# Retention and HGRN2 step: the fourth weight rows' T1, T3 and T4 splits tied behind pair two's token sums, pair three's tokens prepared one product later

## The chip, the cores and the metric

The kernel runs on one core of a Trainium2 chip. The metric is device time in microseconds (us). The kernel before takes 1026.99 us, the median of three runs (1026.68 to 1027.75). Engines are named as in the profile: PE is TensorE with its matmuls, PEld its weight loads, DVE VectorE, ACT ScalarE, POOL GpSimd, and SP the SyncE queue that issues most of the DMA transfers.

## The reference, cut to what matters

One layer with two parallel groups of four heads, retention and HGRN2, on 2048 prompt tokens and 8 sample tokens:

```
h = rmsnorm(x, norm_g)
p = (h @ w_in)                       # (2048, 1024) @ (1024, 8*512)
rq, rk, rv, rg, hq, hf, hi, hgate = split(p, 8)
rq = rotary(rq); rk = rotary(rk) * DK**-0.5
o_ret, s_ret = chunked_decay_recurrence(rq, rk, rv, log_gamma, s_ret)
o_hg,  s_hg  = chunked_decay_recurrence(silu(hq), kin(hf), hi, logf(hf), s_hg)
o = concat(head_rmsnorm(o_ret) * silu(rg), head_rmsnorm(o_hg) * silu(hgate))
y = rmsnorm(x + o @ w_out, final_norm_g)
```

All of it is float32. The work around the change is a part of `h @ w_in`: the 1024 columns of `w_in` that are called `w_v` (two column types of 512), for the first pairs of token chunks.

## The kernel before, in words

A float32 operand is split into a rounded high part (ACT writes it, L117) and the rest (DVE subtracts, L118). The helper is `hi_lo`. A product is three matmuls (high by high, high by low, low by high; `three`, L350) for each of four rows k of 128.

The 2048 tokens are 16 chunks of 128, taken as eight pairs. Pairs zero and one (`plain_k`) multiply the chunks straight, eight rows each. From pair two on (`v_pair`) a pair is one 2 by 2 block product with seven products instead of eight. Its token blocks are A11, A12, A21, A22 and four sums S1 to S4, and its weight blocks are B11, B21, B22 and four sums T1 to T4. The seven products run in the order of `CHAIN`: A11 B11, A12 B21, S2 T2, S1 T1, S3 T3, S4 B22, A22 T4. Products zero, two, four and six add up in one PSUM bank, called `pv2a` for pair two (`pv3a` for pair three). Its running sum is copied out by ACT in between: `s` after product zero and `u` after product two (L390), and `vo` after product four (L402), and PE may add the next product to the bank only when that copy is done. In the same way product three leaves its result in bank `pv2c`, ACT copies it (`p`, L390), and only then product five, S4 B22, may go on in that bank.

The weight sums come from `w_sums` and are made row by row in `wv_comb(0)` to `wv_comb(3)`: four DVE subtractions and four splits for each row. They stand between the end of pair zero and the plain products of pair one.

The tokens of a pair are made ready by `tok_ops` (L302 scales them by the norm, eight DVE instructions of 256 elements; L117 and L118 split them into `ab_h` and `ab_l`, first A11 as 512 elements, then A12 and A22 as 1024; L318 to L321 make the four sums, two in each tile `S`). `s_split(i, 0)` splits S2 and S3, `s_split(i, 1)` splits S1 and S4. Pair two's tokens are prepared beside pair one's last plain products, and pair i+1's tokens inside pair i: `after[n]` is a list of closures that the program emits behind product n. `stats_sum` squares rows of the prompt on ACT (L269, tiles `xn`, which an SP load brings). `decode_values_out` copies the sample tokens' values (`vd`, L615) and is emitted behind product three of pair two.

Each engine works through a fixed list of instructions, in order. The lists are laid down before the run by the framework, which takes the order of emission, the data dependences and its own priorities. The helper `behind(f)` ties what `f` emits: it stands behind the last instruction that DVE, ACT and SP have been given so far.

Of the kernel before, what the change touches and what calls it, by code (L numbers as in the profile page):

```python
# [14 lines left out]
ALU = mybir.AluOpType  # L15
# [26 lines left out]
def step_kernel(ctx, tc, a, out):  # L42
    nc = tc.nc
    pe, act, dve, pool, sp = nc.tensor, nc.scalar, nc.vector, nc.gpsimd, nc.sync
# [71 lines left out]
    def hi_lo(h, l, src):  # L116
        act.activation(h, src, AF.Copy)  # L117
        dve.tensor_tensor(l, src, h.bitcast(F32), op=ALU.subtract)  # L118

    def split(r, name):  # L120
        h = wp.tile([P, D], F32R, tag="wh", name=name + "h")
        l = wp.tile([P, D], F32R, tag="wl", name=name + "l")
        hi_lo(h, l, r)
        return h, l

    def behind(f):

        last = {}
        for i in reversed(nc.cur_bb.bb.instructions):
            if i.engine in (dve.engine, act.engine, sp.engine) and i.engine not in last:  # L130
                last[i.engine] = i
                if len(last) == 3:
                    break
        with ExitStack() as es:
            for i in last.values():
                es.enter_context(tc.issue_after(i))
            f()
# [64 lines left out]
    N_V = len(V_ORDER)  # L202
# [16 lines left out]
    b12 = [[wp.tile([P, 2, GW], F32R, tag="w" + t, name=f"B12{t}{n}") for n in range(2)] for t in "hl"]  # L219

    def wv(op, k):
        if op == "B12":
            return [t[k // 2][:, k % 2] for t in b12]
        return [t[:, k] for t in Bop[op]]
# [3 lines left out]
    def bank(shape, name, at=None):  # L228
        if at is not None:
            return ((ps_pj, ps_lv, ps_o)[at]).tile(shape, F32, tag=("pj", "lv", "o")[at], name=name)  # L230
        pl, tag = ((ps_pj, "pj"), (ps_lv, "lv"), (ps_o, "o"), (ps_tr, "tr"))[(0, 1, 2, 0, 1, 2, 3)[bank_n[0] % 7]]
        bank_n[0] += 1
        return pl.tile(shape, F32, tag=tag, name=name)
# [3 lines left out]
    def tok_load(i):  # L237
        p = TOK[i]
        xr[i] = [rawp.tile([P, 4, 2 * P], F32, tag="raw", name=f"xr{i}{j}") for j in range(2)]
        for j, r in enumerate(xr[i]):  # L240
            src = a_dram[p] if spooled(i) else a["x_t"][p]
            sp.dma_start(r, src[:, 4 * j : 4 * j + 4])
        if spooled(i):
            sraw[i] = [rawp.tile([P, 2, 4, P], F32, tag="raw", name=f"S{n}_{i}") for n in range(2)]
            for n, r in enumerate(sraw[i]):
                sp.dma_start(r, s_dram[p][n])

    def spooled(i):
        return i >= 2 * N_V or (i >= N_V and TOK[i] not in TOK[:2])

    def same(i):
        return 0 < i < len(TOK) and TOK[i] == TOK[i - 1]
# [6 lines left out]
    def stats_load(i, j):  # L259
        c = 2 * V_ORDER[i] + j  # L260
        st[i, j] = [vq.tile([P, GW], F32, tag="xn", name=f"xn{c}{h}", bufs=2) for h in range(2)]
        for h, r in enumerate(st[i, j]):
            sp.dma_start(r, a["x_prompt"][0, c * P : (c + 1) * P, h * GW : (h + 1) * GW])

    def stats_sum(i, j):
        if not j:
            st[i] = sm.tile([P, 4], F32, tag="ms", name=f"ms{V_ORDER[i]}")
        for h, r in enumerate(st[i, j]):
            act.activation(r, r, AF.Square, accum_out=st[i][:, 2 * h + j : 2 * h + j + 1])  # L269
# [7 lines left out]
    def stats_end(i):  # L277
        p, ms = V_ORDER[i], st[i]
        pool.tensor_tensor(ms[:, 0:2], ms[:, 0:2], ms[:, 2:4], op=ALU.add)
        rsqrt_mean(rs_all[:, 2 * p : 2 * p + 2], ms[:, 0:2], D, EPS)  # L280
# [3 lines left out]
    def spread(i):  # L284
        pt = ps_tr.tile([P, 2, P], F32, tag="tr", name=f"prs{i}")
        for j in range(2):
            c = 2 * TOK[i] + j
            pe.transpose(pt[:, j], rs_all[:, c : c + 1].to_broadcast([P, P]), ident)
        dst = vq.tile([P, GW], F32, tag="rq", name=f"rb{i}")[:, :256]
        dve.tensor_copy(dst, pt.rearrange("p a b -> p (a b)"))  # L290
        spread_to[i] = dst
# [36 lines left out]
    def s_split(i, m):  # L328
        hl = split(sraw[i][m].rearrange("p s k t -> p (s k t)"), f"s{i}{m}")
        for n, op in enumerate((("S2", "S3"), ("S1", "S4"))[m]):  # L330
            sop[i, op] = [
                x[:, n * 512 : n * 512 + 512].rearrange("p (k t) -> p k t", k=4) for x in hl
            ]
# [151 lines left out]
    wr = {}  # L485
# [16 lines left out]
    def w_sums(r0, r1):  # L502
        b11, b12, b21, b22 = (r[:, g] if hasattr(r, "shape") else r[g] for r in (r0, r1) for g in range(2))
        dve.tensor_tensor(b11, b12, b11, op=ALU.subtract)
        dve.tensor_tensor(b12, b22, b12, op=ALU.subtract)
        dve.tensor_tensor(b22, b22, b11, op=ALU.subtract)
        dve.tensor_tensor(b21, b21, b22, op=ALU.subtract)
        return ("T2", b22), ("T3", b12), ("T1", b11), ("T4", b21)

    def wv_comb(k):  # L510
        for op, r in w_sums(wr[k], wr[k + 4]):
            h, l = wv(op, k)
            hi_lo(h, l, r)

    def wg_load(n, k):
        for j, kk in enumerate((k, k + 4)):
            if n == 1 and (j or k % 2):
                tags = (f"zh{j}", f"zl{j}") if k % 2 else ("rk", "rg")
                wr[kk] = [vq.tile([P, GW], F32, tag=t, name=f"wgr{n}{kk}{t}") for t in tags]
                for g, r in enumerate(wr[kk]):  # L520
                    sp.dma_start(r, a[f"w_{n}"][kk, :, g * GW : (g + 1) * GW])
            else:
                wr[kk] = rawp.tile([P, 2, GW], F32, tag="raw", name=f"wgr{n}{kk}")
                sp.dma_start(wr[kk].rearrange("p g n -> p (g n)"), a[f"w_{n}"][kk])
# [106 lines left out]
    def plain_out(i, c, ty, ps):  # L631
        cc = 2 * V_ORDER[i] + c
        o = vq.tile([P, GW], F32, tag="vo", name=f"vp{cc}{ty}", bufs=3)
        act.activation(o, ps, AF.Copy, scale=rs_all[:, cc : cc + 1])
        v_out(0, cc, ty, o)

    def plain_k(i, ps, c, ty, k, first, last):
        three(ps, av(i, f"A{c + 1}{k // 4 + 1}", k % 4), wv(f"B{k // 4 + 1}{ty + 1}", k % 4), first, last)
# [46 lines left out]
    wv_comb(1)  # L685
    tok_load(2)
    wv_comb(2)
    wv_comb(3)
    for ty in (1, 0):
        for c in range(2):  # L690
            ps = bank([P, GW], f"pv1{c}{ty}")
            for k in range(KT):
                plain_k(1, ps, c, ty, k, k == 0, k == KT - 1)
            plain_out(1, c, ty, ps)
            if (c, ty) == (0, 0):
                spread(2)
                held = []
                stats_load(3, 0)
                stats_sum(3, 0)
                stats_load(3, 1)  # L700
                tok_ops(2, held, lambda: stats_sum(3, 1))
                stats_end(3)
                tok_load(3)
                for f in held:
                    f()
                s_split(2, 0)
    s_split(2, 1)
    stats_load(4, 0)
    dve.tensor_tensor(lbd, lbraw[:, :, 0], lbraw[:, :, 1], op=ALU.subtract)
    act.activation(lb, lbd, AF.Sigmoid)  # L710
# [208 lines left out]
    for i in range(2, n_tok):  # L919
# [13 lines left out]
        if same(i + 1):  # L933
            for op in ("S1", "S2", "S3", "S4"):
                sop[i + 1, op] = sop[i, op]
        elif i + 1 < n_tok:
            if not spooled(i + 1):
                after[1] += [lambda i=i: spread(i + 1)]
            tied = behind if i >= N_V - 1 else lambda f: f()
            late = 2 if same(i) else 0  # L940
            after[2 + late] += [
                lambda i=i, t=tied: t(lambda: tok_ops(i + 1)), lambda i=i, t=tied: t(lambda: s_split(i + 1, 0))
            ]
            after[4 + late // 2] += [lambda i=i, t=tied: t(lambda: s_split(i + 1, 1))]
        if i + 2 < n_tok and not same(i + 2):
            at = 5 if i % N_V > 2 else 2
            if same(i + 1):
                at = 6
            after[at] += [lambda i=i: tok_load(i + 2)]
# [10 lines left out]
        if m < 3:  # L960
# [9 lines left out]
            if j == 7:  # L970
                after[0] += [lambda m=m: behind(lambda: wg_decode_out(m))]
                for n, (_, op, _) in enumerate(CHAIN):
                    if m == 1 and op == "B11":
                        continue
                    at = {"B21": 0, "B22": 3}.get(op, n) if m == 1 else n
# [25 lines left out]
        if N_V <= i < 2 * N_V:  # L1001
            for n in range(12):
                for f, d in ((lambda n: behind(lambda: wo_pre_load(n)), 0), (lambda n: behind(lambda: wo_pre_split(n)), 2), (lambda n: behind(lambda: wo_pre_store(n)), 4)):
                    g = 7 + 4 * n + d
# [580 lines left out]
    levels, rest, late = [], [], []  # L1585
    tail = r_steps(N_V)
    tail_f = [lambda n=n: [f() for f in tail[n]] for n in sorted(tail)]
    for i in range(len(order)):
# [23 lines left out]
        late = rest  # L1612
# [272 lines left out]
    op = ctx.enter_context(tc.tile_pool(name="op", bufs=1))  # L1885
# [8 lines left out]
    for n in range(4):  # L1894
        i, st_ = ((4, 0), (4, 4), (5, 0), (5, 4))[n]
        wd_at[i] += [(st_, lambda n=n: wd_load(2 * n)), (st_, lambda n=n: wd_load(2 * n + 1))]
        i, st_ = ((4, 3), (5, 0), (5, 4), (6, 1))[n]
# [106 lines left out]
```

## Time and profile before

| what | value |
|---|---|
| median of 3 runs | 1026.99 us |
| profiled execution | 1027.67 us |
| its span, first to last instruction | 1025.8 us |
| PE busy | 1014.7 us, 99% |
| PEld busy | 842.6 us, 82% |
| DVE busy | 734.3 us, 72% |
| ACT busy | 551.5 us, 54% |
| POOL busy | 126.3 us, 12% |
| SP's DMA queue, share of 16 engines | 64.7% |

PE is busy nearly all the time, so the place to read is where it is not: the table of windows shows in which stretch PE has idle time, and the timeline shows which instruction of another engine ended it. A time in the timeline is microseconds from the start of the span.

### The profile page before, as it was taken

The numbers are of one execution on the slowest core, as the hardware profiler recorded it, in microseconds if no ns is written. First come the engines' busy times: TensorE is split into PE (matmuls) and PEld (weight loads), VectorE is DVE, ScalarE is ACT, GpSimd is POOL, SyncE is SP. The second block draws the span as 40 slices with busy tenths as digits, with TensorE's granted clock in tenths as the row PEclk, the third lists the DMA queues.
The fourth block names the chain that finished last, engine by engine and source line by source line (L and its number), as shares of the span: only waits on it lengthen the run. The fifth ranks groups of instructions, "written<-read, shape, count | busy, mean of one in ns | idle before, by whom it ended". The sixth has DMA issues, their size and how long they took to land. (4 is left out here: it accounts for less than half of the span.)

```text
span 1025.8 us, 21565 instructions
## 1 busy us (share of the span) xinstructions
PE 1014.7 (99%) x8372; PEld 842.6 (82%) x8372; DVE 734.3 (72%) x1353; ACT 551.5 (54%) x1211; POOL 126.3 (12%) x231
## 2 busy tenths in 40 slices
PE   9999999999999999999999999999999999999996
PEld 8767778887778888888888899898888878887775
DVE  5897665988675885566666758768768576668886
ACT  6864335735434665555564655666556476433242
POOL 0210101000000101111111100111022112301122
PEclk9999999999999999999999999999999999999999
DMA  8688998768999975677776697655963497566652
GB/s 288 219 303 312 371 341 310 302 251 315 319 323 307 363 250 165 190 244 240 226 239 193 220 328 260 205 178 205 288 205 133 136 350 234 180 254 205 231 183 103
DMA packets 152135, 255.63 MB, mean 249 GB/s; under 512 B 11520, under 2 KB 79376, under 8 KB 151904
## 3 DMA queue, kind: packets, MB, share of 16 engines
q1 hardware_dynamic: 142232, 225.01, 64.7%
q0 software_dynamic: 7440, 24.76, 6.3%
q10 hardware_dynamic: 2360, 4.47, 1.2%
q8 instruction: 66, 1.08, 0.4%
q14 instruction: 37, 0.30, 0.1%
HBM read 166.51 MB, written 87.69 MB: 248 GB/s over the span
## 5 line engine op out<-in xcount | busy, mean ns | idle before, releaser
L1054 PE MATMUL pjfh<-xh,w_h 128*128 128x512 f32 (+2 forms) x160 | 59.4, 371 | 0.0
L1054 PE MATMUL pjqh<-xh,w_h 128*128 128x512 f32 (+2 forms) x160 | 58.7, 367 | 0.0
L1248 ACT ACTIVATE kepth<-kh 128x1024 f32<-128x1024 f32 x24 | 25.4, 1060 | 60.4 <-DVE kh L1238 60.4
L1054 PE MATMUL pjfh<-xl,w_h 128*128 128x512 f32 (+2 forms) x160 | 55.7, 348 | 0.0
L1054 PE MATMUL pjqh<-xh,w_l 128*128 128x512 f32 (+2 forms) x160 | 55.7, 348 | 0.0
L1054 PE MATMUL pjfh<-xh,w_l 128*128 128x512 f32 (+2 forms) x160 | 55.6, 348 | 0.0
L1054 PE MATMUL pjqh<-xl,w_h 128*128 128x512 f32 (+2 forms) x160 | 55.6, 347 | 0.0
L1238 DVE TENSOR_TENSOR kh<-kh,fph 128x512 f32<-128x512 f32 x48 | 33.4, 696 | 22.7 <-PE plh L1268 19.7
L118 DVE TENSOR_TENSOR ab_l<-xr,ab_h 128x512 fp32r<-128x512 f32 (+1 forms) x40 | 37.4, 954 | 14.1 <-ACT ab_h L117 14.1
L783 DVE SCALAR_TENSOR_TENSOR obr<-por,omr,rg 128x128 f32<-128x128 f32 x64 | 18.0, 344 | 31.9 <-POOL omr L775 24.9
L773 ACT ACTIVATE obr<-por 128x128 f32<-128x128 f32 x64 | 16.9, 278 | 44.1 <-PE por L760 40.3
L117 ACT ACTIVATE ab_h<-xr 128x512 fp32r<-128x512 f32 (+1 forms) x40 | 32.3, 839 | 8.4 <-DVE xr L302 8.4
L1054 PEld LDWEIGHTS pjqh<-xh,w_h 128*128 128x128 f32 x160 | 30.4, 190 | 4.8 <-issue 1.2
L1054 PEld LDWEIGHTS pjfh<-xh,w_h 128*128 128x128 f32 x160 | 30.2, 189 | 4.1 <-issue 0.4
L1054 PEld LDWEIGHTS pjqh<-xh,w_l 128*128 128x128 f32 x160 | 30.1, 188 | 4.0
L1054 PEld LDWEIGHTS pjfh<-xh,w_l 128*128 128x128 f32 x160 | 30.1, 188 | 4.0
L409 ACT ACTIVATE vo<-vo 128x512 f32<-128x512 f32 x32 | 20.1, 629 | 23.7 <-DVE vo L403 10.5
L1241 DVE TENSOR_TENSOR qqh<-qqh,fph 128x512 f32<-128x512 f32 x48 | 32.8, 683 | 0.0
L1054 PEld LDWEIGHTS pjqh<-xl,w_h 128*128 128x128 f32 x160 | 30.2, 189 | 3.0
L1054 PEld LDWEIGHTS pjfh<-xl,w_h 128*128 128x128 f32 x160 | 30.2, 189 | 2.7
L302 DVE SCALAR_TENSOR_TENSOR xr<-xr,g_in,rb 128x256 f32<-128x256 f32 x64 | 26.9, 479 | 2.6 <-DMA xr<-in_x_t 2.4
L1681 PE MATMUL py<-woh,oc_h 128*128 128x512 f32 x64 | 26.7, 417 | 0.0
(1877 smaller groups left out, 3347.0 us busy)
## 6 DMA issues: line engine op xcount, KB each, us to landing
xr<-a_dram SPq DMA_DIRECT2D x24, 512.0 KB
S<-s_dram SPq DMA_DIRECT2D x24, 512.0 KB
xn<-in_x_prompt SPq DMA_DIRECT2D x32, 256.0 KB
xr<-in_x_t SPq DMA_DIRECT2D x16, 512.0 KB
a_dram<-xr SPq DMA_DIRECT2D x16, 512.0 KB
s_dram<-S SPq DMA_DIRECT2D x16, 512.0 KB
xr<-a_dram SPq DMA_DIRECT2D x32, 256.0 KB
or<-o_dram SPq DMA_DIRECT2D x16, 512.0 KB
```

The source lines that it names most:

```text
L117: act.activation(h, src, AF.Copy)
L118: dve.tensor_tensor(l, src, h.bitcast(F32), op=ALU.subtract)
L302: dve.scalar_tensor_tensor(r[:, k], r[:, k], g_in[:, kk : kk + 1], spread_to[i], op0=ALU.mult, op1=ALU.mult)
L409: act.activation(o, src, AF.Silu)
L773: act.activation(o[:, cc], po[:, h], AF.Square, scale=P ** -0.5, accum_out=ms[:, h : h + 1])
L783: dve.scalar_tensor_tensor(o[:, cc], po[:, h], ms[:, h : h + 1], rb_of[c, "g"][:, cc], op0=ALU.mult, op1=ALU.mult)
L1054: pe.matmul(ps, ww[:, kk], x[:, k, b0 : b0 + n], start=(k == 0 and i == 0), stop=(k == KT - 1 and i == 2),)
L1238: dve.tensor_tensor(kv[:, :, 0, :], kv[:, :, 0, :], two[:, :, 1:2].to_broadcast([P, nb, b]), op=ALU.mult)
L1241: dve.tensor_tensor(qv[:, :, 1, :], qv[:, :, 1, :], two[:, :, 0:1].to_broadcast([P, nb, b]), op=ALU.mult)
L1248: act.activation(ss[:, 512:], k[:, :HALF], AF.Copy)
L1681: pe.matmul(ps, o[:, kk], w[:, k % 4, i * 512 : (i + 1) * 512], start=(k == 0 and n == 0), stop=(k == KT - 1 and n == 2),)
```

## The change

Two things change. `wv_comb(3)`, the last row of weight sums, is cut in three: the first three subtractions and T2's split stay where they were, T1's split is tied behind `s_split(2, 0)`, and T3's split, the fourth subtraction and T4's split are tied behind `s_split(2, 1)`. And inside pair two, `tok_ops(3)` and `s_split(3, 0)` are emitted behind product three instead of product two, and the load of pair four's tokens behind product three, too. `s_split(3, 1)` stays behind product four.

```
+    def wv_comb_two(k):
+        b11, b12, b21, b22 = (r[:, g] for r in (wr[k], wr[k + 4]) for g in range(2))
+        dve.tensor_tensor(b11, b12, b11, op=ALU.subtract)
+        dve.tensor_tensor(b12, b22, b12, op=ALU.subtract)
+        dve.tensor_tensor(b22, b22, b11, op=ALU.subtract)
+        hi_lo(*wv("T2", k), b22)
+        def one():
+            hi_lo(*wv("T1", k), b11)
+        def two():
+            hi_lo(*wv("T3", k), b12)
+            dve.tensor_tensor(b21, b21, b22, op=ALU.subtract)
+            hi_lo(*wv("T4", k), b21)
+        return one, two
...
-    wv_comb(3)
+    comb_t1, comb_t34 = wv_comb_two(3)
...
                 s_split(2, 0)
+                behind(comb_t1)
     s_split(2, 1)
+    behind(comb_t34)
...
-            late = 2 if same(i) else 0
+            late = 2 if same(i) else 1 if i == 2 else 0
...
-            at = 5 if i % N_V > 2 else 2
+            at = 5 if i % N_V > 2 else 3 if i == 2 else 2
```

No instruction is added or taken away. The lists of PE, POOL and SP keep their order; those of DVE and ACT change between pair one and pair six.

On ACT, around pair two's first copy `s_2` out of bank `pv2a`, the list before was this (the T splits are not in it, they stand earlier):

```order
L117 ACTIVATE s20h<-S_2_710 128x1024
L117 ACTIVATE s21h<-S_2_711 128x1024
L390 ACTIVATE s_2_792<-pv2a 128x512
L269 ACTIVATE xn_763,ms_821<-xn_763 128x512
L117 ACTIVATE ab_h<-xr_719 128x512
L390 ACTIVATE u_2_840<-pv2a 128x512
```

and it is now:

```order
L117 ACTIVATE s20h<-S_2_703 128x1024
L117 ACTIVATE T1h<-wvr_292 128x512
L117 ACTIVATE s21h<-S_2_704 128x1024
L117 ACTIVATE T3h<-wvr_292 128x512
L390 ACTIVATE s_2_792<-pv2a 128x512
L269 ACTIVATE xn_763,ms_821<-xn_763 128x512
L117 ACTIVATE T4h<-wvr_294 128x512
L390 ACTIVATE u_2_840<-pv2a 128x512
```

T1h and T3h stand ahead of `s_2`, T4h behind it, and the first split of pair three's tokens (`ab_h`, 512 elements) has moved further down.

On ACT, from pair two's product two to its product six, before (`p_2` is the copy that S4 B22 waits for, `vo_914<-pv2a` the copy that A22 T4 waits for):

```order
L623 ACTIVATE rbd<-prsd 128x8
L269 ACTIVATE xn_764,ms_821<-xn_764 128x512
L117 ACTIVATE ab_h<-xr_720 128x1024
L390 ACTIVATE p_2_890<-pv2c 128x512
L117 ACTIVATE s30h<-S_3_856 128x1024
L615 ACTIVATE vd_892<-pvd 8x256 x2
L615 ACTIVATE vd_897<-pvd 8x256 x2
L402 ACTIVATE vo_914<-pv2a 128x512
```

and now:

```order
L640 ACTIVATE rbd<-prsd 128x8
L269 ACTIVATE xn_764,ms_821<-xn_764 128x512
L117 ACTIVATE ab_h<-xr_712 128x512
L390 ACTIVATE p_2_860<-pv2c 128x512
L117 ACTIVATE ab_h<-xr_713 128x1024
L117 ACTIVATE s30h<-S_3_876 128x1024
L632 ACTIVATE vd_892<-pvd 8x256 x2
L632 ACTIVATE vd_897<-pvd 8x256 x2
L402 ACTIVATE vo_914<-pv2a 128x512
```

`p_2` has moved ahead of the large `ab_h`, and both `ab_h` stand behind the second `xn`.

On DVE, from the copy `rb` that starts pair three's tokens to the split of their first sums, before:

```order
L290 COPY rb_819<-prs_816 128x256
L302 SCALAR_TENSOR_TENSOR xr_719<-xr_719,g_in,rb_819 128x256 x4
L302 SCALAR_TENSOR_TENSOR xr_720<-xr_720,g_in,rb_819 128x256 x2
L118 TENSOR_TENSOR ab_l<-xr_719,ab_h 128x512
L302 SCALAR_TENSOR_TENSOR xr_720<-xr_720,g_in,rb_819 128x256 x2
L624 TENSOR_TENSOR pk<-pk,rbd 128x64
L318 TENSOR_TENSOR S_3_857<-xr_719,xr_720 128x512
L320 TENSOR_TENSOR S_3_856<-xr_719 128x512
L319 TENSOR_TENSOR S_3_856<-S_3_857,xr_719 128x512
L118 TENSOR_TENSOR ab_l<-xr_720,ab_h 128x1024
L321 TENSOR_TENSOR S_3_857<-xr_720,S_3_856 128x512
L118 TENSOR_TENSOR s30l<-S_3_856,s30h 128x1024
```

and now:

```order
L290 COPY rb_819<-prs_816 128x256
L118 TENSOR_TENSOR T4l<-wvr_294,T4h 128x512
L302 SCALAR_TENSOR_TENSOR xr_712<-xr_712,g_in,rb_819 128x256
L641 TENSOR_TENSOR pk<-pk,rbd 128x64
L302 SCALAR_TENSOR_TENSOR xr_712<-xr_712,g_in,rb_819 128x256 x3
L302 SCALAR_TENSOR_TENSOR xr_713<-xr_713,g_in,rb_819 128x256 x4
L118 TENSOR_TENSOR ab_l<-xr_712,ab_h 128x512
L318 TENSOR_TENSOR S_3_877<-xr_712,xr_713 128x512
L118 TENSOR_TENSOR ab_l<-xr_713,ab_h 128x1024
L319 TENSOR_TENSOR S_3_876<-S_3_877,xr_712 128x512
L320 TENSOR_TENSOR S_3_876<-xr_712 128x512
L321 TENSOR_TENSOR S_3_877<-xr_713,S_3_876 128x512
```

The two sums S2 and S3 (L319, L320), which `s30h` on ACT reads, have moved from ahead of the large `ab_l` to behind it.

## Rows read from the trace of the kernel before

**Rows 1.** Windows: stretch, busy us of PE, PEld, DVE, ACT, POOL; clock, DMA share, GB/s.
```profile
50.00:76.27 26.27, 24.16 (x103) 17.90 (x101) 24.54 (x45) 16.69 (x35) 3.91 (x7) 1.00 0.86 300
76.27:100.00 23.73, 23.73 (x123) 18.52 (x126) 17.41 (x28) 10.13 (x19) 1.08 (x3) 1.00 0.86 304
100.00:1000.00 900.00, 899.80 (x7788) 751.74 (x7781) 639.84 (x1186) 479.28 (x1052) 108.70 (x190) 1.00 0.73 250
```
**Rows 2.** Timeline of PE: start, duration, engine, line, operation; in brackets idle before, releaser.
```profile
56.67 0.50 PE L350 MATMUL pv2a<-wv_h,ab_h 128*128 128x512 f32 x1 [0.90 <-ACT ab_h L117]
...
60.66 0.50 PE L350 MATMUL pv2b<-wv_h,ab_l 128*128 128x512 f32 x1 [0.24 <-DVE ab_l L118]
...
63.79 0.50 PE L350 MATMUL pv2a<-T2h,s20h 128*128 128x512 f32 x1 [0.33 <-ACT s L390]
...
73.25 0.50 PE L350 MATMUL pv2c<-B22h,s21h 128*128 128x512 f32 x1 [0.64 <-ACT p L390]
...
76.27 0.50 PE L350 MATMUL pv2a<-T4h,ab_h 128*128 128x512 f32 x1
```
**Rows 3.** Timeline of ACT, pair two.
```profile
55.99 0.63 ACT L117 ACTIVATE ab_h<-xr 128x512 fp32r<-128x512 f32 x1 [1.57 <-DVE xr L302]
56.53 0.61 ACT L269 ACTIVATE xn<-xn 128x512 f32<-128x512 f32 x1
...
57.14 0.61 ACT L269 ACTIVATE xn<-xn 128x512 f32<-128x512 f32 x1
...
58.18 1.06 ACT L117 ACTIVATE ab_h<-xr 128x1024 fp32r<-128x1024 f32 x1 [0.33 <-DVE xr L302]
...
61.24 1.06 ACT L117 ACTIVATE s20h<-S 128x1024 fp32r<-128x1024 f32 x1 [1.43 <-DVE S L319]
62.21 1.04 ACT L117 ACTIVATE s21h<-S 128x1024 fp32r<-128x1024 f32 x1
63.16 0.58 ACT L390 ACTIVATE s<-pv2a 128x512 f32<-128x512 f32 x1
...
71.04 0.63 ACT L269 ACTIVATE xn<-xn 128x512 f32<-128x512 f32 x1 [2.48 <-DMA xn<-in_x_prompt]
...
71.67 1.04 ACT L117 ACTIVATE ab_h<-xr 128x1024 fp32r<-128x1024 f32 x1
72.62 0.58 ACT L390 ACTIVATE p<-pv2c 128x512 f32<-128x512 f32 x1
73.10 1.05 ACT L117 ACTIVATE s30h<-S 128x1024 fp32r<-128x1024 f32 x1
74.05 1.54 ACT L615 ACTIVATE vd<-pvd 8x256 f32<-8x256 f32 x4
75.61 0.60 ACT L402 ACTIVATE vo<-pv2a 128x512 f32<-128x512 f32 x1
```
**Rows 4.** Timeline of DVE, the end of the weight sums and pair two.
```profile
50.20 0.69 DVE L506 TENSOR_TENSOR wvr<-wvr,wvr 128x512 f32<-128x512 f32 x1
...
53.84 0.41 DVE L290 COPY rb<-prs 128x256 f32<-128x256 f32 x1
...
59.39 1.22 DVE L118 TENSOR_TENSOR ab_l<-xr,ab_h 128x1024 fp32r<-128x1024 f32 x1
60.53 0.68 DVE L319 TENSOR_TENSOR S<-S,xr 128x512 f32<-128x512 f32 x1
...
65.67 2.65 DVE L302 SCALAR_TENSOR_TENSOR xr<-xr,g_in,rb 128x256 f32<-128x256 f32 x6
...
70.97 0.68 DVE L319 TENSOR_TENSOR S<-S,xr 128x512 f32<-128x512 f32 x1
72.75 1.23 DVE L118 TENSOR_TENSOR ab_l<-xr,ab_h 128x1024 fp32r<-128x1024 f32 x1 [1.10 <-ACT ab_h L117]
```
**Rows 5.** Timeline of SP's DMA issues, around the second `xn` of pair two.
```profile
59.84 0.32 SPq L344 DMA_DIRECT2D v_dram<-vp  x1
...
62.34 1.03 SPq L263 DMA_DIRECT2D xn<-in_x_prompt  x1
```

## The prediction

> **What bounds the kernel now.** I read the windows first. From 76.27 to 100 us PE is busy all 23.73 us, and from 100 to 1000 us it is busy for 899.80 of 900 [rows 1]. So the kernel is bound by PE, and nothing behind 76.27 us can swallow a delay of PE or hide a gain: what moves the last product of pair two, A22 T4, moves the end by as much. From 50 to 76.27 us PE is busy for 24.16 of 26.27, so 2.11 us is all the idle time there.
>
> Then PE's timeline. The reader is to see four waits: 0.90 us until pair two's first `ab_h`, 0.24 until `ab_l`, 0.33 until the copy `s`, 0.64 until the copy `p` [rows 2]; they add up to that 2.11. The fifth row, A22 T4 at 76.27, has no idle time in brackets, and yet its first matmul takes the 0.50 us that the four which had waited take. ACT's copy `vo` out of the same bank ends at 75.61 + 0.60 = 76.21, just ahead of it [rows 3]. That copy releases T4 already now, with almost nothing to spare.
>
> Last the timelines of ACT and DVE, to see what each of these waits hangs on.
>
> **The change part by part.** Nothing is added or removed. The sum is over the moment at which A22 T4 starts.
>
> *Fourth weight row.* T1l, the fourth subtraction, T3l and T4l leave DVE ahead of the copy `rb` of 53.84; that is four of about 0.60. DVE does not win all of 2.4 us, since T2l now has to wait for ACT's T2h, which starts when L506 ends (50.20 + 0.69) and takes about 0.62, like the `ab_h` of that size. T2l then starts at about 51.6, and `rb` 0.60 later, at 52.2 instead of 53.84: 1.6 us earlier, or 1.3 if the `xn` ahead of T2h on ACT holds it a little [rows 3, 4]. The first `ab_h` comes at 54.4 to 54.7 instead of 55.99, before PE needs it: the wait of 0.90 goes. The large `ab_h` (58.18) stands behind the `xn` of 57.14, whose landing time the trace doesn't show; it ran without waiting. If it lands as early as ACT can use it, `ab_h` gains 1.6, if not before 57.14, then 0.43. I take 1.2, nearer the early end, since ACT found it landed [rows 3]. The large `ab_l` (59.39), L319 (60.53) and `s20h` (61.24) follow, so about 1.3 us earlier each.
>
> *The same splits, put back.* On ACT, T1h and T3h now stand ahead of `s`. One split of 512 costs 56.53 - 55.99 = 0.54, both 1.08 [rows 3]. So `s` is at 63.16 - 1.3 + 1.08 = 62.9 and PE takes S2 T2 at 63.5 to 63.6 instead of 63.79. Of more than 1 us won, about 0.2 to 0.3 is left there (bounds from the paragraph above: 0.65 lost, 0.6 won). T1l, T3l, the subtraction and T4l land on DVE between `s20l` and pair three's L302, three of them behind `s21l`; `pk` comes forward to behind the first L302 and waits some 0.4 us for `rbd`, which waits for PE. ACT's T1h leaves `s21l` 0.8 of the 1.3 us, and three of 0.60 follow: L302 starts at 65.67 - 0.8 + 1.8 = 66.7, and its eight end at about 70.3 (the six take 2.65, so eight 3.5, and a little for `pk`) [rows 4].
>
> *Pair three's tokens one product later.* The copy `p` now has only `xn` and the small `ab_h` ahead of it. Call X the moment at which ACT can start that second `xn`, whose load the trace shows to have ended ACT's wait at 71.04. Then `p` starts at X + 0.63 + 0.54, which is 0.41 us less behind X than now (72.62 - 71.04 = 1.58), and PE's wait of 0.64 mostly goes. But what is late next is `vo`, and with it A22 T4. `s30h` reads both S2 and S3, which were made at 70.97 and before, ahead of the large `ab_l` [rows 4]; so it could run at 73.10, right behind `p` [rows 3]. Now they stand behind that `ab_l`, which waits for the large `ab_h`, which stands behind `p`. `s30h` waits for all this, and behind it on ACT in strict order stand the four `vd` and then `vo`. Step by step from X, with the start-to-start distances of [rows 2 to 4]:
>
> - `xn` 0.63, small `ab_h` 0.54, `p` 73.10 - 72.62 = 0.48: the large `ab_h` starts at X + 1.65;
> - from it to the large `ab_l` on DVE, 72.75 - 71.67 = 1.08: X + 2.73;
> - `ab_l` 60.53 - 59.39 = 1.14, then L319 0.60 and L320 0.68, and 0.03 to ACT: `s30h` starts at X + 5.18 (now X + 2.06);
> - `s30h` 0.95, the four `vd` 1.56, and from `vo` to T4 76.27 - 75.61 = 0.66: A22 T4 starts at X + 8.35 (now X + 5.23).
>
> So at the same X the change costs 3.12 us at T4. X itself comes earlier: SP issues in order, and the store `vp` at 59.84 waits for ACT's `vp`, which stands right behind the large `ab_h`. The four issues behind it and the load of `xn` at 62.34 follow [rows 5]; SP's order is kept. All move by the 1.2 us that `ab_h` gains. The load takes 8.7 us to land, behind transfers that are shifted alike, so I take X = 71.04 - 1.2 = 69.84 and T4 at 78.2: 1.9 us late. Bounds: X not earlier at all, 3.1 us late; X so early that DVE's L302 decide (they end at 70.3, so the large `ab_h` starts at 70.35, which is X = 68.7), T4 at 77.05, 0.8 us late. Loads that follow on SP are issued some 0.5 us later than now and leave the queue freer, so I lean a little to the early side: 1.8 us.
>
> *What else is late.* `s30l`, `s31h` and `s31l` come 2 to 3 us later than now; PE asks for `s30` only in pair three's product two, which stands behind the whole of A22 T4 and two more products of 2.73 us, over 8 us; so they cost nothing. In pair three the order of `s40h` and `vo` is turned round, too, but there the tokens are not displaced: 0.95 of `s40h` stands against the 2.73 us (twelve matmuls of 0.23) of product five between `vo`'s input and T4. POOL, PE and SP keep their order and cost nothing.
>
> The profiled execution took 1027.67 us (span 1025.8 and 1.87 around it), so the sum for it is 1027.67 + 1.8 = 1029.5. That execution is 0.68 above the median of 1026.99; from the median the forecast is 1028.8 us. Its own range by the bounds is 1027.8 to 1030.1.
>
> **The rivals.**
>
> *A. The waits just go.* If `xn`, `ab_h` and the sums come so early that `vo` is done in time, PE loses nothing: all of 2.11 us [rows 1, 2], giving 1024.9. For it: these four are the only waits, and each of them is relieved. Against it: `s` gets 1.08 us of splits in front, and T4 is now held by a chain of 8.35 us behind X, so X would have to be below 66 and L302 to end 3 us before 70.3. Chance 0.06.
>
> *B. A wash.* X comes early enough, and `pk` and T4l hold DVE less than I think, so that T4 starts within 0.7 us of 76.27; 1026.5 to 1027.7, at the middle 1027.1. It decides where X is under 68.7 and L302 end before 70.2. Not slower, in any way that can be told. Chance 0.13.
>
> *C. PE's clock.* The granted clock is 1.00 (2.4 GHz) in all stretches shown [rows 1], also around the waits, of which the longest is 0.90 us. Here PE would stand idle from the end of S4 B22 (at about 75.3, that is 76.27 less the wait of 0.64 and the 0.3 won before) to T4 at 78.2, some 3 us in one piece, which this trace nowhere shows behind its start. If the grant fell to 1.2 GHz there and stayed so for one product, that product, 76.27 - 73.25 = 3.0 us with its start [rows 2], would take twice as long: 3.0 us more, 1031.8. Chance 0.07. The Trainium skill, "TensorE: Matmul & The Clock Gate", Part 1, says that an idle PE falls to half its clock and has to be kept busy for a time before the full one is given back; no row of before shows a fall.
>
> **How the numbers follow.** Forecast 0.74, A 0.06, B 0.13, C 0.07. A measurement of this kernel can tell about 0.2%, or 2.05 us, from no change. The forecast's 1.8 us lies just inside; of its range 0.8 to 3.1 I put 0.45 above 2.05 and 0.55 below. Slower: 0.74 x 0.45 + 0.07 = 0.40. Same: 0.74 x 0.55 + 0.13 = 0.54. Faster: 0.06. The range from 1027.0 to 1030.4 holds the forecast with its bounds and most of B, and leaves out A and C, 0.13 in all.
>
> **What would show it right or wrong.** In the profile of the changed kernel the first `ab_h` of pair two should start at 54.3 to 54.8 with no wait of PE before it; `s` at 62.5 to 63.3; PE should lose its wait for `p`; and in its place one long wait of 2 to 4 us should stand before A22 T4, released by ACT's `vo`, with `s30h` released by DVE's L320 two to three us later than at 73.10. The second `xn` should end ACT's wait near 69.8; T4 should come 8.35 us behind it. PE should have no wait behind T4. I am wrong if no wait stands before T4, if `s30h` starts before the large `ab_l`, or if PE waits anywhere in pair three or four.

## The result, and the profile after

The changed kernel takes 1031.2 us, the median of 18 runs (1027.36 to 1032.95), against 1027.65 us for the kernel before in the same series (18 runs, 1025.43 to 1030.48). The ratio is 1.0031, with a 95% interval of 1.0022 to 1.0041: slower by 3.2 us (the two medians differ by 3.55). Slower was forecast, but by 1.8 us and to no more than 1030.4.

The profiled execution hides most of it: 1028.26 us, span 1026.4, only 0.6 us above the profiled one of before. Its windows (columns as in [rows 1]):

```profile
50.00:76.27 26.27, 23.62 (x104) 18.45 (x102) 23.31 (x41) 15.20 (x30) 3.25 (x4) 1.00 0.88 316
76.27:100.00 23.73, 22.84 (x112) 18.14 (x113) 18.02 (x30) 11.78 (x24) 2.24 (x6) 1.00 0.93 320
100.00:1000.00 900.00, 899.55 (x7787) 751.20 (x7786) 640.01 (x1186) 478.13 (x1048) 107.36 (x188) 1.00 0.73 249
```

PE's idle time from 50 to 100 us has grown from 2.11 to 3.54 us, and it is one wait now. PE's whole list of waits in the profile after (who waited for whom: total, times, longest, in us):

```profile
PE pv2a L350 <- ACT vo L402: 3.5, 1, 3.5
PE wu L84 <- POOL ones L78: 1.1, 1, 1.1
PE pv8a L350 <- ACT u L390: 0.3, 1, 0.3
```

The four waits of [rows 2] are gone in this trace, and in their place stands one of 3.5 us, by the copy `vo`, before A22 T4. PE's timeline of after has it as its only row with idle time between 54 and 106 us; it is the row that answers to the last one of [rows 2]:

```profile
77.16 0.50 PE L350 MATMUL pv2a<-T4h,ab_h 128*128 128x512 f32 x1 [3.54 <-ACT vo L402]
```

ACT's timeline of after, the rows that answer to [rows 3]:

```profile
52.96 0.63 ACT L117 ACTIVATE ab_h<-xr 128x512 fp32r<-128x512 f32 x1 [0.52 <-DVE xr L302]
...
55.30 1.04 ACT L117 ACTIVATE ab_h<-xr 128x1024 fp32r<-128x1024 f32 x1
...
61.20 0.57 ACT L390 ACTIVATE s<-pv2a 128x512 f32<-128x512 f32 x1
...
68.82 0.63 ACT L269 ACTIVATE xn<-xn 128x512 f32<-128x512 f32 x1 [3.27 <-DMA xn<-in_x_prompt]
...
69.45 0.62 ACT L117 ACTIVATE ab_h<-xr 128x512 fp32r<-128x512 f32 x1
69.97 0.58 ACT L390 ACTIVATE p<-pv2c 128x512 f32<-128x512 f32 x1
70.45 1.05 ACT L117 ACTIVATE ab_h<-xr 128x1024 fp32r<-128x1024 f32 x1
73.99 1.06 ACT L117 ACTIVATE s30h<-S 128x1024 fp32r<-128x1024 f32 x1 [2.50 <-DVE S L320]
74.95 1.53 ACT L632 ACTIVATE vd<-pvd 8x256 f32<-8x256 f32 x4
76.51 0.60 ACT L402 ACTIVATE vo<-pv2a 128x512 f32<-128x512 f32 x1
```

and DVE's, which answer to the last two of [rows 4], now the other way round:

```profile
71.53 1.22 DVE L118 TENSOR_TENSOR ab_l<-xr,ab_h 128x1024 fp32r<-128x1024 f32 x1
72.67 0.68 DVE L319 TENSOR_TENSOR S<-S,xr 128x512 f32<-128x512 f32 x1
73.27 0.68 DVE L320 TENSOR_TENSOR S<-xr 128x512 f32<-128x512 f32 x1
```

The reader is to see the chain of the prediction, link by link: `xn` at X = 68.82, the large `ab_h` at X + 1.63, `ab_l`, L319, L320, then `s30h` at X + 5.17 after an idle ACT of 2.50 us that L320 ended, the four `vd`, `vo`, and A22 T4 at 77.16 = X + 8.34.

But T4 is only 0.89 us later than the 76.27 of before, and the windows hold the full clock. That explains the 0.6 us of this execution and not the 3.2 of the median. What differs is the mean granted clock, which each run lists: 0.998 to 0.999 in the profiled run and one other of the 18, 0.995 to 0.997 in sixteen.

### The profile page after: what moved, and what is told of

Read it like the earlier page. It is cut to its first block, busy times and chain, and to the rows that moved or that the text cites. A ratio compares the mean times of both kernels' runs of the same rounds, so it can differ in the third digit from the quotient of the medians.

```text
span 1026.4 us, 21572 instructions
## 1 busy us (share of the span) xinstructions
PE 1014.1 (99%) x8372; PEld 843.4 (82%) x8372; DVE 734.6 (72%) x1353; ACT 551.9 (54%) x1211; POOL 127.8 (12%) x231
## 4 chain that ended last, share of the span: by engine, by line
PE 92%; DMA 3%; DVE 2%; issue 1%; ACT 1%; SPq 0%; POOL 0%; POOLq 0%; ACTq 0%; DVEq 0%
PE po L350 11%; PE pjqh L1073 9%; PE pjfh L1073 8%; PE py L1700 4%; PE pv L350 4%; PE plh L1287 2%; PE par L764 1%; PE puh L1156 1%; PE pur L771 1%; PE por L777 1%; PE poh L1172 1%; PE por L779 1%; DMA T3l<-ws1T 1%; PE poh L1174 1%; PE pv20a L350 1%; PE pv22a L350 1%
```

## The experiments

Theory 1, clock: the piece of 3.5 us in which PE stands idle makes the clock fall in most runs, which costs some 2 to 3 us on top of the late T4. Theory 2, wait: T4 comes later in most runs than in the profiled one, by a later `xn`. Theory 3: the moved instructions of pairs three to six cost it. In all ratios below, the kernel before is timed in the same series.

**The changed kernel again**, without an edit.

> The changed kernel once more. Clock theory: the wait of 3.5 us before A22 T4 costs about 1 us by itself (0.9 in the first profile), and in most runs the granted clock falls to half behind it for some microseconds; then runs with a mean clock of 0.995 to 0.997 take 2 to 4 us more than those at 0.998 or 0.999, and a profile of such a run shows a stretch behind 75 us with a granted clock well under 1. Wait theory: the wait itself is longer in most runs because the xn load lands later (2 to 3 us more), the clock of all stretches stays at 1.00, and the time follows the wait.

Measured: 1030.6 us (12 runs), ratio 1.0027 [1.0018, 1.0035]. The clock is 0.994 to 0.997 in ten runs and 0.998 in two; all 29 runs of before lie at 0.998 or 0.999. The profiled run is one at 0.998 (1027.99 us): wait 3.5 us, X at 69.50, T4 at 77.84. So the wait has the same length again, and the clock goes with the time by and large, but the trace of a fall was still missing.

**The wait filled on PE, lightly.** `fill` is emitted behind product five.

```
+    def fill():
+        pt = ps_tr.tile([P, P], F32, tag="tr", name="fill")
+        for _ in range(7):
+            pe.matmul(pt, ones, ones, start=True, stop=True)
...
+            after[5] += [fill]
```

> The changed kernel with seven matmuls of 128x128 by ones, about 2.8 us, put on PE between S4 B22 and A22 T4; they compute nothing that is used. Clock theory: A22 T4 starts when it did (8.35 us behind xn), PE is kept busy, the mean clock is 0.998 to 0.999 in all runs, and the time is 0.5 to 2 us above before, not 3.2. Wait theory: the fill changes nothing, ratio 1.003 again. A third theory, that the moved instructions of pairs three to six cost it: 1.003 too.

Measured: 1030.11 us (11 runs), ratio 1.0029 [1.0017, 1.0041]. A miss for theory 1 as put. The fill took 1.7 us and not 2.8 and left PE a wait of 1.97 us; six of the eleven runs still list 0.996 or 0.997, where theory 1 had expected none; its profile is of a run at 0.999. By the ratio alone this run would have spoken for theories 2 and 3, so the fill had to be made longer and denser.

**The wait filled densely.** The same place, product five once more into a spare bank that nobody reads:

```
+        for k in range(4):
+            (xh, xl), (wh, wl) = av(2, "S4", k), wv("B22", k)
+            for x, w in ((xh, wh), (xh, wl), (xl, wh)):
+                pe.matmul(pt, x, w, start=True, stop=True)
```

> The changed kernel with twelve matmuls of 128x512 (2.7 us), product five over again into a spare bank that nobody reads, between S4 B22 and A22 T4. They leave PE under 1 us of the wait of 3.5. Clock theory (PE's idle piece brings the clock down): all runs at a mean clock of 0.998 or 0.999, T4 where it was, so the time is that of the changed kernel's undisturbed clock, 1028 to 1029, ratio 1.0005 to 1.0015. Other theory (the clock falls for a reason that is not PE's idle time): most runs at 0.995 to 0.997 and ratio 1.0025 to 1.003 as for the changed kernel.

Measured: 1029.3 us (11 runs), ratio 1.0013 [1.0005, 1.0022]. The clock is 0.998 or 0.999 in eight runs (1028.8 us in the mean) and 0.997 in three (1030.0), where theory 1 had expected all at 0.998 or 0.999. PE's row of T4 in its profile:

```profile
77.83 0.50 PE L350 MATMUL pv2a<-T4h,ab_h 128*128 128x512 f32 x1 [0.72 <-ACT vo L402]
```

T4 starts where it does without the fill (X there is 69.48, so X + 8.35). Up to T4 the lists of ACT and DVE are those of the changed kernel, and what differs is that PE was busy; behind T4 some of their instructions in pairs three to seven have changed places, without a wait of PE there. Over half of the loss is gone. Theory 2 would have left it at 1.003, and so would theory 3 if those places don't matter.

**The wait made longer.** Each of the four `vd` copies is made three times.

```
+                for _ in range(3):
+                    act.activation(t[:, n * 256 : n * 256 + 256], pvd[0][32 * j : 32 * j + NB], AF.Copy)
```

> The changed kernel with each copy of the sample values made three times, which puts some 3.3 us more of ACT's work ahead of vo; the wait before A22 T4 grows from 3.5 to about 6.9 us. Clock theory: the clock falls in every run, also in the profiled one, whose windows behind the wait show a granted clock of about half for some microseconds; mean clock 0.994 to 0.996, time 3.3 us over that of the changed kernel's runs with a fallen clock: 1034 to 1035, ratio 1.006 to 1.007. Without an effect of the clock: 1027.6 + 1 + 3.3 = 1032, ratio 1.004, all windows at 1.00.

Measured: 1033.87 us (4 runs), ratio 1.0057 [1.0035, 1.0079], clock 0.993 to 0.995 in all four. The interval holds the 1.004 without an effect of the clock, too, so here the windows decide and not the time. The wait is 6.4 us, not 6.9, since five of the twelve `vd` copies have come out behind `vo`. PE stands idle from 72.56 to 78.99. The clock is 1.00 until 76 us, 0.51 in the microsecond behind that, 0.50 until 82 and 1.00 again from 83, some 4 us after PE had taken up its work.

**The changed kernel profiled three times more**, to see the fall in its own trace.

> The changed kernel, one look, to catch the fall of the clock in its own trace. Clock theory: where the mean clock is 0.995 to 0.997, the windows behind the wait show a stretch of 5 to 8 us with a granted clock of about 0.5, PE takes twice as long for the products in it, and A22 T4 starts where it does in the looks without a fall (X + 8.35, 77 to 78.2). Other theory: in such a run T4 starts 2 us later and all windows are at 1.00.

> The same look at the changed kernel once more, since not every run shows the fall; both theories expect what they expect of the first look.

> A third look at the changed kernel, for the same reason; both theories expect what they expect of the first look.

Measured: 1030.9, 1030.55 and 1028.08 us, clock 0.995, 0.997 and 0.998. T4 starts at 77.38, 77.46 and 77.70, each 8.34 or 8.35 us behind its X (69.04, 69.12, 69.35), and the wait is 3.5 us in each. PE's row of T4 in the first of the three traces, and its windows (columns as in [rows 1]):

```profile
77.38 0.80 PE L350 MATMUL pv2a<-T4h,ab_h 128*128 128x512 f32 x1 [3.55 <-ACT vo L402]
```

```profile
74.00:75.00 1.00, 0.00 (x0) 0.00 (x0) 0.78 (x2) 0.79 (x1) 0.00 (x0) 1.00 0.56 229
75.00:76.00 1.00, 0.00 (x0) 0.00 (x0) 0.70 (x1) 0.96 (x4) 0.00 (x0) 1.00 1.02 418
76.00:77.00 1.00, 0.00 (x0) 0.00 (x0) 1.00 (x3) 0.96 (x3) 0.00 (x0) 0.68 1.01 414
77.00:78.00 1.00, 0.62 (x2) 0.52 (x3) 0.95 (x2) 1.00 (x2) 0.00 (x0) 0.50 1.10 266
78.00:79.00 1.00, 1.00 (x4) 0.81 (x3) 0.75 (x2) 1.00 (x4) 0.00 (x0) 0.50 1.01 201
...
82.00:83.00 1.00, 1.00 (x7) 0.27 (x9) 0.00 (x0) 0.00 (x0) 0.00 (x0) 0.50 1.04 404
83.00:84.00 1.00, 1.00 (x17) 0.26 (x9) 0.38 (x1) 0.00 (x0) 0.00 (x0) 0.91 0.77 295
```

Windows of the third trace:

```profile
76.00:77.00 1.00, 0.00 (x0) 0.00 (x0) 1.00 (x2) 0.96 (x3) 0.00 (x0) 1.00 1.03 422
77.00:78.00 1.00, 0.30 (x1) 0.30 (x2) 0.94 (x3) 0.98 (x3) 0.00 (x0) 1.00 1.07 340
78.00:79.00 1.00, 1.00 (x6) 0.79 (x5) 0.74 (x2) 1.00 (x2) 0.00 (x0) 1.00 1.35 229
```

The column to read is the granted clock, third from the end. In the first trace PE stands idle from 73.83; the clock is 1.00 (2.4 GHz) until 76, 0.68 in the row behind that, then 0.50 (1.2 GHz) until 83. In the third, with as long a wait, it stays at 1.00. PE is busy in all of the first trace's rows from 78 us on, yet starts four matmuls between 78 and 79 where the third starts six, and T4's first matmul takes 0.80 us instead of 0.50. The 0.68 and 0.91 put the two turns at about 76.4 and 83.2 us. From T4 at 77.38 to 83.2 that is 5.8 us of work at half clock, half of which is lost: 2.9 us by this estimate. The spans of the first and third trace differ by 1029.1 - 1026.3 = 2.8. In the second trace the clock falls at about 77.4, as T4 starts, and is back by 80.9, after 3.4 us; by the same estimate that costs 1.7. A later row bears both out: ACT's last copy of pair six, `vo` (L407), which PE releases. In the first, the second and the third trace:

```profile
165.10 0.60 ACT L407 ACTIVATE vo<-pv6a 128x512 f32<-128x512 f32 x1 [3.90 <-PE pv6a L350]
```

```profile
164.11 0.60 ACT L407 ACTIVATE vo<-pv6a 128x512 f32<-128x512 f32 x1 [3.89 <-PE pv6a L350]
```

```profile
162.81 0.60 ACT L407 ACTIVATE vo<-pv6a 128x512 f32<-128x512 f32 x1 [3.89 <-PE pv6a L350]
```

It starts 87.7 us behind T4 in the first, 86.6 in the second and 85.1 in the third, as in the other two traces in which the clock held. So the fall has cost 2.6 and 1.5 us up to there.

That is rival C, seen directly, and theory 2 is out: T4 doesn't start later in the two traces with a fall. Over the 33 runs of the changed kernel the clock fell in 28 (0.997 or less), which took 1031.0 us in the mean, and held in 5, with 1028.3. The line at 0.997 is not sharp: 2 of the 71 runs of before list 0.997, too, at 1026.8 and 1025.4 us. The six such runs of the changed kernel take 1030.9 us, like the rest of the 28; for the filled kernels the listed mean is all there is.

Theory 3 falls by the same runs. The instructions of pairs three to six are moved in all 33, and yet five take 1028.3 us; and the 85.1 us from T4 to the end of pair six are not more than the 85.2 in the trace of before:

```profile
161.50 0.60 ACT L407 ACTIVATE vo<-pv6a 128x512 f32<-128x512 f32 x1 [1.71 <-PE pv6a L350]
```

**One part alone: the later tokens.** The fourth row is back to `wv_comb(3)`.

> Only pair three's tokens are moved one product later; the splits of the fourth weight row stay where they were before the change. The lists of ACT and DVE come out nearly as before: s30h reads sums made ahead of the large ab_l again, and p stands behind the large ab_h. If the wait before A22 T4 is a matter of both parts together: no long wait, T4 at 76 to 76.5, the four waits of before, clock 0.998 to 0.999, ratio 0.999 to 1.001. If the later tokens make the wait by themselves: T4 at 78, ratio 1.002 to 1.003.

Measured: 1026.89 us (11 runs), ratio 0.9998 [0.9988, 1.0008], clock 0.998 or 0.999. T4 at 75.55, earlier than the 76 to 76.5 expected, as X is at 70.33; it is X + 5.22, as before. Of the four waits two are there, `s` with 0.32 us and `p` with 0.99. By itself this part changes nothing: ACT's list comes out as before, and DVE's but for `pk`.

**One part alone: the splits.** The two numbers that move pair three's tokens and load are back.

```
-            late = 2 if same(i) else 1 if i == 2 else 0
+            late = 2 if same(i) else 0
...
-            at = 5 if i % N_V > 2 else 3 if i == 2 else 2
+            at = 5 if i % N_V > 2 else 2
```

> Only the splits of the fourth weight row are moved; pair three's tokens are prepared where they were before the change. The order on ACT that comes out has vo ahead of s30h, behind three of the four vd and the large ab_h: T4 at X + 4.3, no wait of over 0.5 us before it, ratio 0.998 to 0.999 (1 to 2 us under before). If the loss came from the splits in front of the copy s: S2 T2 at 64.5 or later and a ratio of 1.001 or more.

Measured: 1025.84 us (12 runs), ratio 0.9979 [0.9967, 0.9991], clock 0.998 or 0.999. S2 T2 at 61.66, T4 at 73.65 with hardly a wait (X is 69.36, so X + 4.29), `s` 0.69 us late. ACT's rows:

```profile
71.53 1.04 ACT L117 ACTIVATE ab_h<-xr 128x1024 fp32r<-128x1024 f32 x1
72.59 0.38 ACT L632 ACTIVATE vd<-pvd 8x256 f32<-8x256 f32 x1
73.00 0.60 ACT L402 ACTIVATE vo<-pv2a 128x512 f32<-128x512 f32 x1
73.49 1.05 ACT L117 ACTIVATE s30h<-S 128x1024 fp32r<-128x1024 f32 x1
```

`vo` has come out ahead of `s30h`. So the splits win what they can win, and the wait belongs to the pair of edits and to neither alone.

**The order of `vo` and `s30h` turned round.** The changed kernel with one number altered:

```
-            after[3] += [lambda: behind(decode_values_out)]
+            after[4] += [lambda: behind(decode_values_out)]
```

> The changed kernel with the sample values' copies (vd) emitted behind product four instead of three; that turns the order of vo and s30h on ACT round, too. Both theories on T4: no wait of over 0.5 us before A22 T4, T4 at about 74.5 to 75.5, no fall of the clock, and the time 1 to 2 us under before (ratio 0.998 to 0.999). If the loss lies in pairs three to six: ratio 1.001 to 1.003.

> The kernel with the sample values' copies one product later, again, for its time: ratio 0.9965 to 0.9990 as before, mean clock 0.998 or 0.999 in all runs, A22 T4 at 73 to 75 without a wait. If the first 6 runs were luck: 0.999 to 1.000.

Measured: 1025.27 us (6 runs), ratio 0.9976 [0.9963, 0.9989], and in a second series 1025.87 us (11 runs), 0.9985 [0.9976, 0.9994]; the clock is 0.998 or 0.999 in all 17. `vo` follows the large `ab_h` at once, and T4 starts without a wait (first series):

```profile
70.21 1.05 ACT L117 ACTIVATE ab_h<-xr 128x1024 fp32r<-128x1024 f32 x1
71.16 0.59 ACT L402 ACTIVATE vo<-pv2a 128x512 f32<-128x512 f32 x1
73.76 1.06 ACT L117 ACTIVATE s30h<-S 128x1024 fp32r<-128x1024 f32 x1 [2.01 <-DVE S L320]
```

```profile
73.22 0.39 PE L350 MATMUL pv2a<-T4h,ab_h 128*128 128x512 f32 x1
```

This version beats both kernels, by 1.2 to 2.3 us under before. It is no test of theory 3: from 84 us on its lists of ACT and DVE are again those of the kernel before, as they are with the splits alone.

**One step more: the splits behind `s`.** As the kernel before it, and both calls tied behind product zero of pair two:

```
+            after[0] += [lambda: behind(comb_t1), lambda: behind(comb_t34)]
```

> As the kernel with the sample values' copies one product later, and the splits of the fourth row tied behind pair two's product zero, so that the copy s stands ahead of T1h and T3h on ACT. Theory: the wait of 0.5 us before S2 T2 goes as well, T4 at 72.8 to 74.5, ratio 0.997 to 0.998, 0 to 0.6 us under that kernel. Rival: T1l or T4l come too late for products three and six, or pk and L302 get later and the wait before S4 B22 grows; ratio 0.998 to 0.999.

Measured: 1025.84 us (11 runs), ratio 0.9982 [0.9970, 0.9993]. The wait for `s` is gone, T4 comes at 73.05, but the time is not under that of the version above. The list of waits shows one place where it is lost again:

```profile
PE pv7a L350 <- ACT vo L402: 0.9, 1, 0.9
```

Pair seven's A22 T4 waits for its own `vo` here; it did so by 1.35 us with the splits alone, and by 0.94 in the second profile of the version above. In the first profile of that version it doesn't wait, with T4 of pair two as early as 73.22. There ACT had stood idle before this `vo` for 0.57 us until the store `v_dram<-vo` had ended, in the second for 1.80. So when PE runs ahead, that copy takes a part back in some runs; it wasn't tried further.

## Why the prediction was wrong, point by point

*The wait that takes the others' place: right.* The forecast was one wait of 2 to 4 us before A22 T4, released by `vo`, with `s30h` held by L320 behind the large `ab_l`. It is there, 3.5 us long, in every trace of the changed kernel. T4 was put at X + 8.35; five traces show 8.34 or 8.35.

*X: right in kind, too small in size.* It was taken 1.2 us earlier, at 69.84, and came 1.5 to 2.2 us earlier, at 68.8 to 69.5; the large `ab_h`, on which that 1.2 rests, came 2.9 us earlier in the profile after (55.30). T4, forecast for 78.2, came at 77.2 to 77.8. So the term "T4 late by 1.8 us" measured 0.9 to 1.6 against the one trace of before. The time agrees: the five runs with a held clock take 1028.3 us, 0.7 above the 1027.6 of before, and the densely filled wait costs 1.3.

*The four waits: right for two, half right for two.* The waits for `ab_h` and `ab_l` are gone in all five traces. `ab_h` at 52.96 came earlier than the 54.3 to 54.8 that I gave; the weight sums of that run ended 1.6 us sooner (L519 at 48.58 against L506 at 50.20 [rows 4]). `s` started at 60.6 to 62.0, ahead of the forecast 62.5 to 63.3, and yet cost a wait of 0 to 1.3 us from trace to trace, since PE came earlier, too. The wait for `p`, which was to go, is there in three of the five, with 0.2 to 0.75 us. Only the profile after shows neither.

*The step that failed: the chance of rival C.* The sum put nothing in for PE's clock. I had the rival's place, its mechanism and about its price: 3.0 us, where 28 fallen against 5 held runs show 2.7 and the two traces 2.6 and 1.5. I gave it 0.07; it happens in 28 of 33 runs. The mistake was to read the granted clock of 1.00 in all stretches shown, also around the waits, as evidence on a wait of 3 us, when the longest wait in those rows was 0.90 us. Those rows could not speak on it, but the end of the same trace could, which the prediction's "no row of before shows a fall" passes over. PE's last matmul there ends at 1018.1, and behind it the clock falls:

```profile
1020.00:1025.80 5.80, 0.00 (x0) 0.00 (x0) 1.42 (x3) 0.88 (x3) 0.95 (x2) 0.77 0.41 159
```

The row's 0.77 is 1.00 until 1023 and 0.50 from 1024 on. So the fall itself could be read from before, though not how likely it was in a wait of 3 us. The Trainium skill, "TensorE: Matmul & The Clock Gate", Part 1, says that a PE which stands idle falls to half its clock; the traces agree, with 0.50 in the windows above and at that end. Forecast 1028.8 plus C is what was measured: 0.7 to 1.3 us for the late T4, and 2.7 for the clock in 0.85 of the runs, 2.3 in the mean, together 3.0 to 3.6 against the measured 3.2.

*Rivals A and B* did not come. A's reason against it held: `vo` came 7.7 us behind X. What would have made A come true is the order of two instructions on ACT, and one number turns it.

*Pairs three and four: right.* Their products show no wait of PE of 0.2 us or more in any profile of the changed kernel. A small one shows in pair eight in two of the five (0.2 and 0.3 us), where the forecast had none behind T4.

Left open: why the lightly filled kernel's five runs with a held clock take 1029.6 us in the mean and not the 1028.3 of the changed kernel. Its profile has a wait that no other trace shows at that size (1.3 us late in the program, put down to issue); whether it belongs to the fill was not tried. Open, too, is what makes the clock fall in one run and hold in the next, with the same wait.

## What to carry to other kernels

A wait of the engine that bounds the kernel can have a second price when it is one long piece: four waits of 2.1 us in all left the clock at 1.00, one of 3.5 us brought it down in 28 of 33 runs, which then cost some 2.7 us more behind its end. So ask of a change not only how much idle time it leaves, but whether it puts it in one place. And before a producer is moved later, look at what stands behind its consumer in the same engine's list: here the cheap copy that PE waited for stood behind a split that had been made late.

## What the runs showed of the hardware that was not expected

The fall is a matter of single runs: with the same wait of 3.5 us, the clock fell in the third of the three later traces not at all, in the first for some 6.8 us and in the second for some 3.4 us, and a wait of 6.4 us brought it down in all four runs. With a light fill that left 1.97 us of idle time 6 of 11 runs still list a mean of 0.996 or 0.997, with the dense one that left 0.72 us 3 of 11 list 0.997; no trace of these shows the fall. And a single profile can sit on the rare side: the first two profiles of the changed kernel were both of runs in which the clock held. In all, it held in three of the five profiled runs and in two of the 28 others; whether that is chance was not tried. The listed clock of the timed runs, not the trace, gave the cause away.
